# The sample's MLP up-projection with seven block products instead of eight, summed in PSUM

## The chip, the cores and the metric

The kernel runs on one NeuronCore of a Trainium2 chip. The metric is the device time of one execution in microseconds (us). The kernel before takes 2704.45 us (median of 3 runs, 2704.23 to 2707.36). The execution that the profiler recorded took 2709.24 us, of which 2707.5 us lie between its first and its last instruction.

## The reference

One encoder layer is applied to two sequences, a prompt of 512 tokens and a sample of 1024 tokens, with the same weights. Each sequence goes through an input projection, three token mixers, an output projection and an MLP. The change concerns the MLP of the sample alone:

```
D_MODEL, D_FF = 1024, 4096
def rmsnorm(x, w):
    return x * rsqrt(mean(x * x) + EPS) * w
...
x = x + mix @ w_out                                  # output projection
h = rmsnorm(x, norm_mlp_w)
x = x + square(relu(h @ w_up)) @ w_down              # the MLP
...
return rmsnorm(x, norm_f_w)                          # at the end of the trunk
```

All tensors are float32.

## The kernel before

**Products.** A float32 product is made of three passes: each operand is split into a high part (a copy rounded to the type `fp32r`) and a low part (the rest), and `unit` adds high x high, high x low and low x high into one PSUM tile of 128 x 512. Features lie on the partitions, tokens along the row; the sample's 1024 tokens are two blocks `b` of 512. One output tile with 1024 input features takes 8 x 3 = 24 matmuls of 128x512, one with 512 input features 12.

**Weights.** `wtile` loads 512 KB (or 256 KB) of weights by a DMA from the SyncE queue (SP) into a tile `wst` (two buffers), and `piece` splits each 128 x 512 quarter megabyte into a tile `w` (six buffers): ScalarE (ACT) writes the high part, VectorE (DVE) or GpSimd (POOL) the low part.

**The MLP before** (`tail`). After the output projection (tiles `op`, operands `m`) the residual x stands in `x2`. `norm_split` multiplies x by the norm's weight and splits it into eight operands `h` for each block; the factor 1/rms (`rr`, tiles `nacc`, `nsq`, `nps`) is not in them, it is multiplied in later. Then eight rounds `fb` follow: four up-projection tiles (`mu`) for each block, each 24 matmuls; `relu2` and `split` turn each into an operand `a`; and eight down-projection tiles (`md`) for each block, 12 matmuls each, are added onto x by DVE. In the last round the second block is done in two halves of 256 tokens, so that the final norm overlaps.

**Order.** Code records operations with a serial number; a planner (`schedule`) then lets every engine, whenever it is free by the planner's own costs, take the ready operation with the lowest number (`key`). The result is one fixed order for each engine, and each engine runs it strictly in that order, waiting on semaphores. Operations that need a buffer become ready only when one of its ring is free: `q4` (36 buffers of 128 x 1024; x, `h`, `m`, `a`), `w`, `wst`, `e` (11 buffers of 128 x 512 for intermediate results), and the PSUM rings `d` (3 banks) and `m` (5 banks).

The profile names one helper line for nearly every instruction (L592 before, L593 in the changed kernel), so groups are told apart by the tile names.

Of the kernel before, what the change touches and what calls it, by code (L numbers as in the profile page):

```python
# [9 lines left out]
F32 = mybir.dt.float32  # L10
F32R = mybir.dt.float32r
# [5 lines left out]
P = 128  # L17
D = 1024
KT = 8
# [3 lines left out]
WHOLE, HALVES = (slice(0, 512),), (slice(0, 256), slice(256, 512))  # L23
XN = 7
QN = 18
GDN_SHARE = 0.75
FIRST = 8


# [566 lines left out]
def kernel(ctx, tc, xp_t, xs_t, w_in, w_out, w_up, w_down, par, up, out_p, out_s):  # L596
    rec = Rec()
# [19 lines left out]
    def dram(shape, name):  # L617
        return V.of(Buf(name, shape, F32, real=dp.tile(list(shape), F32, name=name)))
# [25 lines left out]
    def mm(o, l, r, start=True, stop=True, **kw):  # L644
        PE.matmul(o, l, r, start=start, stop=stop, **kw)
# [4 lines left out]
    def copy(o, i, **kw):  # L650
        ACT.activation(o, i, AF.Copy, **kw)

    def tt(e, o, a, b, op):
        e.tensor_tensor(o, a, b, op=op)
# [3 lines left out]
    def stt(o, a, sc, b, op0, op1):  # L658
        DVE.scalar_tensor_tensor(o, a, sc, b, op0=op0, op1=op1)
# [38 lines left out]
    def mkseq(name, x, out, n):  # L698
        s = Seq()
        s.name, s.x, s.out, s.n = name, x, out, n  # L700
        s.C, s.nb = n // P, n // 512
        s.raw = [dram([P, n], f"raw_{name}_{g}") for g in range(NG)]
        s.mix = [dram([P, n], f"mix_{name}_{g}") for g in range(16)]
        s.lsd = [dram([P, n], f"lsd_{name}_{h}") for h in range(4)]
        s.rbs = [dram([P, n], f"rbs_{name}_{g}") for g in range(2)]
        s.cumd = dram([64, n], f"cumd_{name}")
        s.shr = [dram([P, s.C, 2, P], f"shr_{name}_{h}") for h in range(4)]
        s.pkd = [[dram([P, s.C, 4, P], f"pkd_{name}_{h}_{d}") for d in range(2)] for h in range(4)]
        s.nd = [[dram([P, s.C, P], f"nd_{name}_{h}_{d}") for d in range(2)] for h in range(4)]
        s.zt = [dram([2, s.C, 4, 32, 32], f"zt_{name}_{h}") for h in range(4)]  # L710
        s.xt = [dram([2, s.C, 4, 32, 32], f"xt_{name}_{h}") for h in range(4)]
        s.et = const([P, 4, 2, s.C], f"et_{name}")
        s.colt = const([P, s.C, 4, 24], f"col_{name}")
        s.ecol = const([P, s.C, 2, 8], f"ecol_{name}")
        s.neg = const([P, s.C, 2, 4], f"neg_{name}")
        return s


    def piece(src, ring="w"):
        w = rec.tile(ring, [P, 2, 512], F32R, "w")  # L720
        split(src, w, ANY)
        return w

    def wtile(src, nk=KT, ring="w"):
        st = rec.tile("wst", [P, nk * P], F32, "wst")
        SP.dma_start(st, src)
        return [piece(st[:, k:k + 512], ring) for k in range(0, nk * P, 512)]

    def split(src, hl, e):
        copy(hl[:, 0, :], src)  # L730
        tt(e, hl[:, 1, :], src, hl[:, 0, :].bitcast(F32), SUB)
# [11 lines left out]
    def unit(ps, w, hs, nk=KT, z=slice(0, 512)):  # L743
        n = 0
        for k in range(nk):
            a, b = (w[k // 4][:, i, k % 4 * P:(k % 4 + 1) * P] for i in range(2))
            hh, hl = hs[k][:, 0, z], hs[k][:, 1, z]
            for l, r in ((a, hh), (a, hl), (b, hh)):
                mm(ps, l, r, n == 0, n == 3 * nk - 1)
                n += 1  # L750
# [11 lines left out]
    def rms(src, sums=((DVE, (0, 1, 2, 3, 4, 5, 6)), (DVE, (7,))), n=512):  # L762
        part = lambda name: tmp(name)[:, 0:n]
        acc = []
        for e, ks in sums:
            a = part("nacc")
            act(a, src(ks[0]), AF.Square)
            for k in ks[1:]:
                sq = part("nsq")
                act(sq, src(k), AF.Square)  # L770
                tt(e, a, a, sq, ADD)
            acc.append(a)
        ps = psd("nps")[:, 0:n]
        mm(ps, ones, acc[0], True, False)
        mm(ps, ones, acc[1], False, True)
        rsq(ps, acc[0], 1.0 / D, room=acc[1])
        return acc[0]

    def norm_split(src, wcol, r=None):
        out = []  # L780
        for k in range(KT):
            h = tmp("nh")
            if r is None:
                DVE.tensor_scalar(h, src(k), col(wcol + k), None, op0=MUL)
            else:
                stt(h, src(k), col(wcol + k), r, MUL, MUL)
            hl = rec.tile("q4", [P, 2, 512], F32R, "h")
            split(h, hl, ANY)
            out.append(hl)
        return out  # L790
# [628 lines left out]

    def tail(s):
        blk = range(s.nb)
        sl = lambda b: slice(b * 512, (b + 1) * 512)
        x2 = [[rec.tile("q4", [P, 2, 512], F32, "x2") for _ in range(4)] for _ in blk]
        xk = lambda b, k: x2[b][k // 2][:, k % 2, :]
        for hf in range(2):
            rbs, hh = [], []
            for b in blk:  # L1430
                if hf:
                    rbs.append(rec.tile("q4", [P, 2, 512], F32, "rb"))
                    for g in range(2):
                        SP.dma_start(rbs[b][:, g, :], s.rbs[g][:, sl(b)])
                hh.append([])
                for k in range(KT):
                    f = tmp("mf")
                    SP.dma_start(f, s.mix[hf * 8 + k][:, sl(b)])
                    if hf:
                        stt(f, f, hn[:, 2 + k:3 + k], rbs[b][:, k // 4, :], MUL, MUL)  # L1440
                    m = rec.tile("q4", [P, 2, 512], F32R, "m")
                    split(f, m, ANY)
                    hh[b].append(m)
            for og in range(KT):
                w = wtile(w_out[hf, og])
                for b in blk:
                    ps = psd("op")
                    unit(ps, w, hh[b])
                    if hf == 0:
                        SP.dma_start(xk(b, og), s.x[og, :, sl(b)])  # L1450
                    tt(DVE, xk(b, og), xk(b, og), ps, ADD)

        h2, rr = [], []
        for b in blk:
            h2.append(norm_split(lambda k: xk(b, k), C_NMLP))
        for b in blk:
            rr.append(rms(lambda k: xk(b, k)))
        ends = [(b, z) for b in blk for z in (HALVES if b else WHOLE)]
        for fb in range(8):
            acts = [[] for _ in blk]  # L1460
            for f in range(4):
                w = wtile(w_up[4 * fb + f])
                for b in blk:
                    ps = psd("mu")
                    unit(ps, w, h2[b])
                    r = tmp("mr")
                    relu2(r, ps, rr[b])
                    a = rec.tile("q4", [P, 2, 512], F32R, "a")
                    split(r, a, ANY)
                    acts[b].append(a)  # L1470

            parts = [[(b, WHOLE[0]) for b in blk]] if fb < 7 else [[e] for e in ends]
            ws = {}
            for part in parts:
                for og in range(KT):
                    if og not in ws:
                        ws[og] = wtile(w_down[fb // 2, og, :, fb % 2 * 512:fb % 2 * 512 + 512], nk=4,
                                       ring="q4" if fb == 7 and og >= 4 else "w")
                    for b, z in part:
                        ps = psd("md")[:, 0:z.stop - z.start]  # L1480
                        unit(ps, ws[og], acts[b], 4, z)
                        tt(DVE, xk(b, og)[:, z], xk(b, og)[:, z], ps, ADD)
        with shifted(-200):
            rs = [rms(lambda k: xk(b, k)[:, z], ((DVE, (0, 4, 1, 5, 2, 6)), (DVE, (3, 7))), z.stop - z.start) for b, z in ends]
        for (b, z), r in zip(ends, rs):
            n = z.stop - z.start
            for k in range(KT):
                v = xk(b, k)[:, z]
                DVE.tensor_scalar(v, v, col(C_NF + k), None, op0=MUL)
            for k in range(KT):  # L1490
                v = xk(b, k)[:, z]
                tt(ANY, v, v, r, MUL)
                if k % 2:
                    SP.dma_start(s.out[k - 1:k + 1, :, b * 512 + z.start:b * 512 + z.stop].rearrange("k p t -> p k t"),
                                 x2[b][k // 2][:, :, z])

    def relu2(r, z, rr):
        stt(r, z, 0.0, rr, ALU.max, MUL)
        act(r, r, AF.Square)
# [46 lines left out]
    with lane("mix"):  # L1546
# [2 lines left out]
            next(g)  # L1549
        for _ in turns((one_by_one(g, gdn(ss_)), GDN_SHARE), (one_by_one(others(sp_), others(ss_)), 1.0)):  # L1550
            pass
    tail(sp_)
    tail(ss_)

    order, _ = schedule(rec)
    left = ctx.enter_context(tc.tile_pool(name="left", bufs=1))
# [112 lines left out]
```

## Time and profile before

| | us |
|---|---|
| median of 3 runs | 2704.45 |
| the profiled execution | 2709.24 |
| its span, first to last instruction | 2707.5 |
| TensorE (PE) busy | 2588.8 (96%) |
| DVE busy | 1758.3 (65%) |
| ACT busy | 1344.5 (50%) |
| sample's MLP, from the first `mu` to the last matmul | 1993.8 to about 2697.5 |

A busy PE in this profile means that matmuls follow each other without a gap; a matmul's own duration is longer than the distance to the next, because they are pipelined. What one matmul costs is therefore read from the distance of starts. The clock in the rows is the TensorE clock that was granted, as a share of 2.4 GHz.

### The profile page before, as it was taken

The numbers are of one execution on the slowest core, as the hardware profiler recorded it, in microseconds if no ns is written. First come the engines' busy times: TensorE is split into PE (matmuls) and PEld (weight loads), VectorE is DVE, ScalarE is ACT, GpSimd is POOL, SyncE is SP. The second block draws the span as 40 slices with busy tenths as digits, with TensorE's granted clock in tenths as the row PEclk, the third lists the DMA queues.
The fourth block names the chain that finished last, engine by engine and source line by source line (L and its number), as shares of the span: only waits on it lengthen the run. The fifth ranks groups of instructions, "written<-read, shape, count | busy, mean of one in ns | idle before, by whom it ended". The sixth has DMA issues, their size and how long they took to land. (4 is left out here: it accounts for less than half of the span.)

```text
span 2707.5 us, 39889 instructions
## 1 busy us (share of the span) xinstructions
PE 2588.8 (96%) x13992; PEld 2080.0 (77%) x13992; DVE 1758.3 (65%) x3235; ACT 1344.5 (50%) x2691; POOL 319.8 (12%) x623
## 2 busy tenths in 40 slices
PE   8999999989999999999999999999999999999998
PEld 6778777767767777677787788888888888888887
DVE  7997557989885558788997576565543333333336
ACT  6863448878855348776656455442331222122222
POOL 0110002323231012223121000000000000000001
PEclk9999999999999999999999999999999999999999
DMA  6796667666654677677645563462111111111112
GB/s 227 235 294 198 194 187 234 190 198 193 182 184 136 199 225 224 197 224 227 193 128 154 176 186 105 148 229 89 55 39 47 55 47 43 51 51 51 47 47 71
DMA packets 271145, 403.60 MB, mean 149 GB/s; under 512 B 48480, under 2 KB 124384, under 8 KB 270944
## 3 DMA queue, kind: packets, MB, share of 16 engines
q1 hardware_dynamic: 270944, 401.05, 47.3%
q8 instruction: 111, 1.82, 0.3%
q14 instruction: 90, 0.74, 0.1%
HBM read 299.11 MB, written 101.84 MB: 148 GB/s over the span
## 5 line engine op out<-in xcount | busy, mean ns | idle before, releaser
L592 PE MATMUL ip<-h,w 128*128 128x512 f32 x3384 | 865.4, 405 | 10.3 <-ACT h L592 7.4
L592 PEld LDWEIGHTS ip<-h,w 128*128 128x128 f32 x3384 | 628.8, 191 | 156.5 <-issue 12.1
L592 ACT ACTIVATE w<-wst 128x512 fp32r<-128x512 f32 x508 | 318.8, 629 | 679.6 <-PE md L592 312.9
L592 PE MATMUL md<-a,w 128*128 128x512 f32 (+1 forms) x2400 | 542.4, 383 | 2.3 <-ACT a L592 2.0
L592 PE MATMUL mu<-h,w 128*128 128x512 f32 x2304 | 540.3, 393 | 0.0
L592 PEld LDWEIGHTS md<-a,w 128*128 128x128 f32 x2400 | 434.9, 188 | 89.5 <-ACT a L592 3.4
L592 PEld LDWEIGHTS mu<-h,w 128*128 128x128 f32 x2304 | 431.0, 188 | 90.4 <-issue 1.2
L592 DVE TENSOR_TENSOR w<-wst,w 128x512 fp32r<-128x512 f32 x503 | 352.9, 703 | 142.9 <-ACT w L592 141.1
L592 DVE TENSOR_TENSOR x<-x,md 128x512 f32<-128x512 f32 (+1 forms) x200 | 132.8, 665 | 226.7 <-PE md L592 226.0
L592 PE MATMUL op<-m,w 128*128 128x512 f32 x1152 | 268.4, 392 | 0.0
L592 PEld LDWEIGHTS op<-m,w 128*128 128x128 f32 x1152 | 214.9, 188 | 47.0 <-issue 2.6
L592 DVE SCALAR_TENSOR_TENSOR cy<-cx,taps,cy 128x512 f32<-128x512 f32 x264 | 202.5, 792 | 6.4 <-ACT cy L592 2.9
L592 DVE SCALAR_TENSOR_TENSOR mr<-mu,nacc 128x512 f32<-128x512 f32 x96 | 66.2, 690 | 154.5 <-PE mu L592 154.3
L592 POOL TENSOR_TENSOR x<-x,nacc 128x512 f32<-128x512 f32 (+1 forms) x11 | 13.4, 1245 | 1053.6 <-DVE nacc L592 1053.6
L592 ACT ACTIVATE mr<-mr 128x512 f32<-128x512 f32 x96 | 60.6, 631 | 152.8 <-DVE mr L592 148.6
L592 DVE TENSOR_TENSOR a<-mr,a 128x512 fp32r<-128x512 f32 x96 | 66.6, 695 | 75.7 <-ACT a L592 75.4
L592 POOL TENSOR_SCALAR_AFFINE_SELECT E<-E 128x512 f32<-128x512 f32 x96 | 78.6, 826 | 181.4 <-DMA E<-cumd_s 101.0
L592 ACT ACTIVATE E<-E,col_s 128x128 f32<-128x128 f32 x256 | 82.1, 392 | 27.0 <-POOL E L592 26.8
L592 ACT ACTIVATE ev<-ip 128x512 f32<-128x512 f32 x94 | 55.5, 591 | 60.0 <-PE ip L592 53.8
L591 ACT ACT_TABLE_LOAD x62 | 79.5, 1283 | 1.1
L592 DVE SCALAR_TENSOR_TENSOR S<-S,dec,ds 64x64 f32<-64x64 f32 x256 | 61.1, 280 | 11.1 <-ACT S L592 4.2
L592 DVE TENSOR_TENSOR x<-x,op 128x512 f32<-128x512 f32 x48 | 32.8, 683 | 54.3 <-PE op L592 54.2
(243 smaller groups left out, 3071.6 us busy)
## 6 DMA issues: line engine op xcount, KB each, us to landing
wst<-in_w_in_dram SPq DMA_DIRECT2D x94, 512.0 KB, 4.4
wst<-in_w_up_dram SPq DMA_DIRECT2D x64, 512.0 KB, 3.5
wst<-in_w_down_dram SPq DMA_DIRECT2D x128, 256.0 KB, 2.6
raw_s<-ev SPq DMA_DIRECT2D x94, 256.0 KB, 2.7
E<-cumd_s SPq DMA_DIRECT2D x64, 256.0 KB, 5.0
pk<-pkd_s SPq DMA_DIRECT2D x64, 256.0 KB, 4.0
wst<-in_w_out_dram SPq DMA_DIRECT2D x32, 512.0 KB, 3.6
raw_p<-ev SPq DMA_DIRECT2D x47, 256.0 KB, 2.4
```

Of the source, the lines that this page charges most:

```text
L591: nc.scalar.preload_act_table_set(o.load)
L592: getattr(getattr(nc, o.eng), o.meth)(*[conv(x) for x in o.args], **{k: conv(x) for k, x in o.kw.items()})
```

## The change

The sample's up-projection is done by a scheme of Strassen's kind. The operands of one pair of output tiles (`q`, 16 of them) are seen as a 2 x 2 block matrix on each side: the weights in output tiles 2q and 2q+1 and in input features 0 to 511 and 512 to 1023 (a11, a12, a21, a22), the activations in input features 0 to 511 and 512 to 1023 and in the two token blocks. Seven products of half the input features (12 matmuls each) take the place of eight. Sums and differences of the operands are made first: on the side of the activations once (`t1` to `t4`, beside the plain blocks `11`, `21` and `22`), on the side of the weights for each q (`s1`, `s2`, a21-a11, a12-s2).

Three PSUM tiles carry the products of one q. X takes the product 11, is copied out as `p1`, and then goes on adding the product 21. W takes t1, is read by DVE (W + p1), and goes on adding 22. Y takes t2, is read, goes on adding t3, is read, goes on adding t4, and is read. The four sums are output tiles and go to DRAM (`z`). For three q the part of X is done first (`AHEAD_Q`), while the operands t1 to t4 are still being made. The residual x goes to DRAM as well (`xr`), to free buffers. Afterwards `z` and `xr` are read back, `relu2` and `split` follow, and the down-projection runs in rounds of 8, 8, 8, 4 and 4 input tiles in place of eight rounds of 4. The output projection's loop takes the outputs in the order 0, 4, 1, 5, 2, 6, 3, 7. The prompt's tail stays as it was, in a function of its own.

```diff
+AHEAD_Q = 3
...
+        if s.nb == 2:
+            s.z = [dram([P, n], f"z_{name}_{f}") for f in range(32)]
+            s.xr = dram([8, P, n], f"xr_{name}")
...
-    def tail(s):
+    def out_proj(s, ogs=range(KT)):
...
-            for og in range(KT):
+            for og in ogs:
...
+        return x2, xk
...
-        for fb in range(8):
-            acts = [[] for _ in blk]
-            for f in range(4):
-                w = wtile(w_up[4 * fb + f])
-                for b in blk:
-                    ps = psd("mu")
-                    unit(ps, w, h2[b])
...
+    def tail_sample(s):
+        blk = range(2)
+        sl = lambda b: slice(b * 512, (b + 1) * 512)
+        x2, xk = out_proj(s, (0, 4, 1, 5, 2, 6, 3, 7))
+        wn = lambda k: col(C_NMLP + k)
+        h = {x: [] for x in ("11", "21", "t1", "t2", "t3", "22", "t4")}
+
+        def part(x, v, k=None):
+            hl = rec.tile("q4", [P, 2, 512], F32R, "h")
+            if k is None:
+                split(v, hl, DVE)
+            else:
+                copy(hl[:, 0, :], v, scale=wn(k))
+                stt(hl[:, 1, :], v, wn(k), hl[:, 0, :].bitcast(F32), MUL, SUB)
+            h[x].append(hl)
+
+        for k in range(4):
+            part("11", xk(0, k), k)
+            part("21", xk(0, k + 4), k + 4)
+
+        def prod(ps, w, x, first=False, last=False):
+            n = 0
+            for k in range(4):
+                a, b = (w[:, i, k * P:(k + 1) * P] for i in range(2))
+                hh, hl = h[x][k][:, 0, :], h[x][k][:, 1, :]
+                for l, r in ((a, hh), (a, hl), (b, hh)):
+                    mm(ps, l, r, first and n == 0, n == 11, skip_group_check=True)
+                    n += 1
+
+        def raw(f):
+            r = rec.tile("wst", [P, KT * P], F32, "wst")
+            SP.dma_start(r, w_up[f])
+            return r[:, 0:512], r[:, 512:1024]
+
+        def put(f, b, v):
+            SP.dma_start(s.z[f][:, sl(b)], v)
+
+        def corner(q, a11, a12):
+            X = psd("mu")
+            prod(X, piece(a11), "11", True)
+            p1 = tmp("p1")
+            copy(p1, X)
+            return p1, X
+
+        def corner2(q, X, a12):
+            prod(X, piece(a12), "21", last=True)
+            v = tmp("z")
+            copy(v, X)
+            put(2 * q, 0, v)
+
+        ahead = []
+        for q in range(AHEAD_Q):
+            a11, a12 = raw(2 * q)
+            p1, X = corner(q, a11, a12)
+            corner2(q, X, a12)
+            ahead.append(p1)
+
+        for k in range(4):
+            x11, t1, t2, t3, t4 = (tmp(x) for x in ("x11", "t1", "t2", "t3", "t4"))
+            copy(x11, xk(0, k), scale=wn(k))
+            stt(t1, xk(1, k), wn(k), x11, MUL, SUB)
+            part("t1", t1)
+            stt(t2, xk(1, k + 4), wn(k + 4), t1, MUL, SUB)
+            part("t2", t2)
+            tt(DVE, t3, x11, t2, SUB)
+            part("t3", t3)
+            part("22", xk(1, k + 4), k + 4)
+            stt(t4, xk(0, k + 4), wn(k + 4), t2, MUL, SUB)
+            part("t4", t4)
+        rr = [rms(lambda k: xk(b, k)) for b in blk]
+        for b in blk:
+            for k2 in range(4):
+                SP.dma_start(s.xr[2 * k2:2 * k2 + 2, :, sl(b)].rearrange("k p t -> p k t"), x2[b][k2])
+
+        for q in range(16):
+            a11, a12 = raw(2 * q)
+            a21, a22 = raw(2 * q + 1)
+            if q < len(ahead):
+                p1 = ahead[q]
+            else:
+                p1, X = corner(q, a11, a12)
+            s1, s2 = tmp("s1"), tmp("s2")
+            W, Y = psm([P, 512], "mu"), psm([P, 512], "mu")
+            tt(ANY, s1, a21, a22, ADD)
+            prod(W, piece(s1), "t1", True)
+            t, u = tmp("z"), tmp("z")
+            tt(DVE, t, W, p1, ADD)
+            tt(ANY, s2, s1, a11, SUB)
+            prod(Y, piece(s2), "t2", True)
+            tt(DVE, u, Y, p1, ADD)
+            if q >= len(ahead):
+                corner2(q, X, a12)
+            tt(ANY, a21, a21, a11, SUB)
+            prod(Y, piece(a21), "t3")
+            tt(DVE, t, Y, t, ADD)
+            put(2 * q + 1, 1, t)
+            tt(ANY, a12, a12, s2, SUB)
+            prod(W, piece(a12), "22", last=True)
+            tt(DVE, u, W, u, ADD)
+            put(2 * q, 1, u)
+            prod(Y, piece(a22), "t4", last=True)
+            tt(DVE, p1, Y, p1, ADD)
+            put(2 * q + 1, 0, p1)
+
+        x2 = [[None] * 4 for _ in blk]
+        xk = lambda b, k: x2[b][k // 2][:, k % 2, :]
+        ends = [(b, z) for b in blk for z in (HALVES if b else WHOLE)]
+        for f0, nf in ((0, 8), (8, 8), (16, 8), (24, 4), (28, 4)):
+            acts = []
+            for b in blk:
+                acts.append([])
+                for f in range(f0, f0 + nf):
+                    v = tmp("av")
+                    SP.dma_start(v, s.z[f][:, sl(b)])
+                    relu2(v, v, rr[b])
+                    a = rec.tile("q4", [P, 2, 512], F32R, "a")
+                    split(v, a, ANY)
+                    acts[b].append(a)
+
+            end = f0 == 28
+            groups = ([[(b, og, WHOLE[0]) for b in blk for og in (g, g + 1)] for g in range(0, KT, 2)] if not end else
+                      [[(b, og, z) for og in range(KT)] for b, z in ends])
+            ws = {}
+            for group in groups:
+                for b, og, z in group:
+                    if f0 == 0 and x2[b][og // 2] is None:
+                        x2[b][og // 2] = rec.tile("q4", [P, 2, 512], F32, "x2")
+                        SP.dma_start(x2[b][og // 2], s.xr[og:og + 2, :, sl(b)].rearrange("k p t -> p k t"))
+                    if og not in ws:
+                        ws[og] = wtile(w_down[f0 // 8, og, :, f0 % 8 * P:(f0 % 8 + nf) * P], nk=nf,
+                                       ring="q4" if end and og >= 4 else "w")
+                    ps = psd("md")[:, 0:z.stop - z.start]
+                    unit(ps, ws[og], acts[b], nf, z)
+                    tt(DVE, xk(b, og)[:, z], xk(b, og)[:, z], ps, ADD)
+        ending(s, x2, ends)
...
-    tail(sp_)
-    tail(ss_)
+    tail_prompt(sp_)
+    tail_sample(ss_)
```

Three places in the order of the engines show how the planner places this.

ACT around the end of the sample's output projection, before: the squares for the norm (`nsq`, `nacc`) stand between the splits of weights (`w`) and operands (`h`) that the last output tiles need.

```order
L592 ACTIVATE nsq_19972<-x_3507_18819 128x512
L592 ACTIVATE w_19984<-wst_19867 128x512
L592 ACTIVATE w_20000<-wst_19867 128x512
L592 ACTIVATE h_20006<-nh_19974 128x512
L592 ACTIVATE nsq_20012<-x_3511_18853 128x512
L592 ACTIVATE h_20023<-nh_20015 128x512
L592 ACTIVATE nacc_20048<-x_3507_18819 128x512
L592 ACTIVATE h_20055<-nh_20050 128x512
```

The same engine in the changed kernel, after the output projection; `mu_20178` is X of the third q done ahead, `w_20263` the high part of the first s1.

```order
L593 ACTIVATE p_3681_20214<-mu_20178 128x512
L593 ACTIVATE nsq_20216<-x_3505_18676 128x512
L593 ACTIVATE z_20231<-mu_20178 128x512
L593 ACTIVATE nsq_20239<-x_3506_18462 128x512
L593 ACTIVATE nsq_20242<-x_3506_18462 128x512
L593 ACTIVATE nsq_20245<-x_3507_18761 128x512
L593 ACTIVATE nacc_20247<-x_3507_18761 128x512
L593 ACTIVATE nacc_20250<-x_3508_18428 128x512
L593 ACTIVATE nsq_20253<-x_3508_18428 128x512
L593 ACTIVATE nsq_20255<-x_3509_18719 128x512
L593 ACTIVATE nsq_20260<-x_3509_18719 128x512
L593 ACTIVATE w_20263<-s_3744_20233 128x512
```

The squares have moved behind the output projection and behind X's copies, in one run, and the first split of s1 stands behind them.

PE at the same place, before: from the last output-projection tile to the norm's sums over partitions (`nps`) and the first up-projection tile.

```order
L592 MATMUL op_20040<-m_19435,w_19851 128x512 x3
L592 MATMUL nps_20076<-nacc_19518,ones 128x512
L592 MATMUL nps_20076<-nacc_20048,ones 128x512
L592 MATMUL nps_20085<-nacc_19557,ones 128x512
L592 MATMUL nps_20085<-nacc_20083,ones 128x512
L592 MATMUL mu_20096<-h_19525,w_19911 128x512 x3
```

PE in the changed kernel, from the end of X of the third q (60 matmuls behind the output projection up to there, then the twelve of its second product) to W (`mu_20268`) and Y (`mu_20299`) of the first q.

```order
L593 MATMUL mu_20178<-h_19621,w_20107 128x512 x3
L593 MATMUL mu_20178<-h_19775,w_20107 128x512 x3
L593 MATMUL mu_20178<-h_20020,w_20107 128x512 x3
L593 MATMUL mu_20178<-h_20079,w_20107 128x512 x3
L593 MATMUL nps_20257<-nacc_20172,ones 128x512
L593 MATMUL nps_20257<-nacc_20247,ones 128x512
L593 MATMUL mu_20268<-h_19598,w_20263 128x512 x3
L593 MATMUL mu_20268<-h_19751,w_20263 128x512 x3
L593 MATMUL mu_20268<-h_20046,w_20263 128x512 x3
L593 MATMUL mu_20268<-h_20091,w_20263 128x512 x3
L593 MATMUL mu_20299<-h_19669,w_20291 128x512 x2
L593 MATMUL nps_20305<-nacc_20250,ones 128x512
```

The norm's sums now stand between the products done ahead and the first W.

DVE in the middle of the up-projection, before: `relu2` of one tile, the low part of a weight piece, the low part of an operand `a`.

```order
L592 SCALAR_TENSOR_TENSOR mr_21330<-mu_21288,nacc_19557 128x512
L592 TENSOR_TENSOR w_21326<-wst_21268,w_21326 128x512
L592 TENSOR_TENSOR a_21342<-mr_21330,a_21342 128x512
L592 SCALAR_TENSOR_TENSOR mr_21364<-mu_21324,nacc_19518 128x512
L592 TENSOR_TENSOR a_21373<-mr_21364,a_21373 128x512
```

DVE in the changed kernel, twelve of the sixteen instructions of one q in the middle: `mu_20743` is W, `mu_20763` Y, `wst_20738` and `wst_20760` hold the weights of the next q.

```order
L593 TENSOR_TENSOR z_20769<-mu_20743,p_3803_20745 128x512
L593 TENSOR_TENSOR w_20765<-wst_20738,w_20765 128x512
L593 TENSOR_TENSOR z_20786<-mu_20763,p_3803_20745 128x512
L593 TENSOR_TENSOR s_3822_20791<-wst_20760 128x512
L593 TENSOR_TENSOR w_20782<-wst_20738,w_20782 128x512
L593 TENSOR_TENSOR s_3823_20799<-s_3822_20791,wst_20738 128x512
L593 TENSOR_TENSOR wst_20760<-wst_20760,wst_20738 128x512
L593 TENSOR_TENSOR wst_20738<-wst_20738,s_3823_20799 128x512
L593 TENSOR_TENSOR w_20808<-s_3822_20791,w_20808 128x512
L593 TENSOR_TENSOR z_20769<-mu_20763,z_20769 128x512
L593 TENSOR_TENSOR w_20823<-s_3823_20799,w_20823 128x512
L593 TENSOR_TENSOR z_20786<-mu_20743,z_20786 128x512
```

The readings of W and Y stand between sums and splits for the next q, and the one that splits the next a11 (`w_20765`) stands ahead of the first reading of Y.

Over the whole program the lists have 11,638 matmuls in place of 11,830, 3,390 DVE instructions in place of 3,237, 2,789 on ACT in place of 2,693 and 1,619 on SP in place of 1,496. PE's list is the same up to the first tile of the sample's output projection.

## Rows read from the trace of the kernel before

**Rows 1.** Page, part 1: busy us, share of the span, instructions.

```profile
PE 2588.8 (96%) x13992; PEld 2080.0 (77%) x13992; DVE 1758.3 (65%) x3235; ACT 1344.5 (50%) x2691; POOL 319.8 (12%) x623
```

**Rows 2.** Windows: us; busy PE, PEld, DVE, ACT, POOL; clock; DMA share; GB/s.

```profile
1900.00:1994.00 94.00, 94.00 (x411) 76.64 (x409) 48.68 (x79) 31.56 (x52) 0.00 (x0) 1.00 0.15 47
1994.00:2650.00 656.00, 656.00 (x2895) 543.01 (x2894) 252.10 (x370) 159.51 (x253) 0.00 (x0) 1.00 0.15 48
2650.00:2707.50 57.50, 45.64 (x288) 40.68 (x286) 42.21 (x90) 14.65 (x30) 10.07 (x9) 0.91 0.21 74
```

**Rows 3.** Waits of PE after 1700 us: total us, times, longest.

```profile
PE nps L592 <- DVE nacc L592: 1.9, 1, 1.9
PE md L592 <- ACT a L592: 1.2, 1, 1.2
```

**Rows 4.** Timeline of PE from 1900 us: start, duration, tiles, count.

```profile
1899.63 91.29 PE L592 MATMUL op<-m,w 128*128 128x512 f32 x402
1990.76 3.60 PE L592 MATMUL nps<-nacc,ones 128*128 128x512 f32 x8
...
2037.74 43.68 PE L592 MATMUL md<-a,w 128*128 128x512 f32 x192
...
2603.50 43.68 PE L592 MATMUL mu<-h,w 128*128 128x512 f32 x192
```

**Rows 5.** Groups of PE by form, 1994 to 2698 us: busy, mean ns, idle.

```profile
L592 PE MATMUL md<-a,w 128*128 128x512 f32 (+1 forms) x1632 | 352.5, 377 | 0.0
L592 PE MATMUL mu<-h,w 128*128 128x512 f32 x1536 | 349.9, 389 | 0.0
```

**Rows 6.** Groups of DVE by form, from 1800 us.

```profile
L592 DVE TENSOR_TENSOR w<-wst,w 128x512 fp32r<-128x512 f32 x158 | 109.1, 692 | 41.4 <-ACT w L592 41.2
L592 DVE TENSOR_TENSOR x<-x,md 128x512 f32<-128x512 f32 x126 | 86.6, 688 | 186.2 <-PE md L592 186.2
```

**Rows 7.** Groups of ACT by form, from 1800 us.

```profile
L592 ACT ACTIVATE nsq<-x 128x512 f32<-128x512 f32 x24 | 15.1, 631 | 41.9 <-DVE x L592 41.5
...
L592 ACT ACTIVATE nacc<-nps,eps 128x512 f32<-128x512 f32 x4 | 2.8, 690 | 2.8 <-PE nps L592 2.8
```

**Rows 8.** Timeline of DVE before the end of the output projection.

```profile
1981.74 0.68 DVE L592 TENSOR_TENSOR h<-nh,h 128x512 fp32r<-128x512 f32 x1
1982.34 0.68 DVE L592 TENSOR_TENSOR nacc<-nacc,nsq 128x512 f32<-128x512 f32 x1
1982.95 0.69 DVE L592 TENSOR_TENSOR h<-nh,h 128x512 fp32r<-128x512 f32 x1
...
1990.96 0.69 DVE L592 TENSOR_TENSOR x<-x,op 128x512 f32<-128x512 f32 x1 [1.37 <-PE op L592]
```

**Rows 9.** Timeline of ACT in the same stretch.

```profile
1980.75 0.64 ACT L592 ACTIVATE h<-nh 128x512 fp32r<-128x512 f32 x1
1981.29 0.62 ACT L592 ACTIVATE nsq<-x 128x512 f32<-128x512 f32 x1
1981.92 0.63 ACT L592 ACTIVATE h<-nh 128x512 fp32r<-128x512 f32 x1
```

**Rows 10.** DMA issues: queue, count, KB each, median us to landing.

```profile
wst<-in_w_up_dram SPq DMA_DIRECT2D x64, 512.0 KB, 3.5
...
raw_s<-ev SPq DMA_DIRECT2D x94, 256.0 KB, 2.7
...
mf<-mix_s SPq DMA_DIRECT2D x32, 256.0 KB, 5.6
```

**Rows 11.** Timeline of PE at 72 us.

```profile
72.15 0.66 PE L592 MATMUL tp<-ident,cy 128*128 128x128 f32 x4 [2.77 <-DVE cy L592]
72.56 3.60 PE L592 MATMUL ip<-h,w 128*128 128x512 f32 x8
```

**Rows 12.** Window at this place, columns as in rows 2.

```profile
72.00:76.00 4.00, 3.85 (x13) 3.08 (x14) 4.00 (x8) 4.00 (x11) 0.27 (x4) 0.59 0.47 165
```

More of the change, by code (lines that the diff above doesn't have):

```diff
@@ L1451, in tail, with ending @@
                     tt(DVE, xk(b, og), xk(b, og), ps, ADD)
-        h2, rr = [], []
-        for b in blk:
[L1455 to L1458, printed above, removed]
-        for fb in range(8):
-            acts = [[] for _ in blk]
-            for f in range(4):
-                w = wtile(w_up[4 * fb + f])
-                for b in blk:
-                    ps = psd("mu")
-                    unit(ps, w, h2[b])
[L1466 to L1482, printed above, removed]
+        return x2, xk
+    def ending(s, x2, ends):
+        xk = lambda b, k: x2[b][k // 2][:, k % 2, :]
         with shifted(-200):
@@ L1485, in tail @@
         for (b, z), r in zip(ends, rs):
-            n = z.stop - z.start
             for k in range(KT):
@@ L1495, in tail, with tail_prompt @@
                                  x2[b][k // 2][:, :, z])
+    def tail_prompt(s):
+        x2, xk = out_proj(s)
+        h2 = norm_split(lambda k: xk(0, k), C_NMLP)
+        rr = rms(lambda k: xk(0, k))
+        for fb in range(8):
+            acts = []
+            for f in range(4):
+                w = wtile(w_up[4 * fb + f])
+                ps = psd("mu")
+                unit(ps, w, h2)
+                r = tmp("mr")
+                relu2(r, ps, rr)
+                a = rec.tile("q4", [P, 2, 512], F32R, "a")
+                split(r, a, ANY)
+                acts.append(a)
+            for og in range(KT):
+                w = wtile(w_down[fb // 2, og, :, fb % 2 * 512:fb % 2 * 512 + 512], nk=4)
+                ps = psd("md")
+                unit(ps, w, acts, 4)
+                tt(DVE, xk(0, og), xk(0, og), ps, ADD)
+        ending(s, x2, [(0, WHOLE[0])])
@@ new lines, in tail_sample @@
+    def tail_sample(s):
[92 more added lines that the diff above has]
+        x2 = [[None] * 4 for _ in blk]
+        xk = lambda b, k: x2[b][k // 2][:, k % 2, :]
+        ends = [(b, z) for b in blk for z in (HALVES if b else WHOLE)]
+        for f0, nf in ((0, 8), (8, 8), (16, 8), (24, 4), (28, 4)):
+            acts = []
+            for b in blk:
[4 more added lines that the diff above has]
+                    relu2(v, v, rr[b])
+                    a = rec.tile("q4", [P, 2, 512], F32R, "a")
+                    split(v, a, ANY)
[16 more added lines that the diff above has]
+        ending(s, x2, ends)
```

## The prediction

> **What bounds the kernel now.** I read the page's shares first: PE 96% busy, DVE 65% [rows 1]. Then the windows of the sample's tail: from 1900 to 2650 us PE is busy for 750 us of 750, at full clock, while DVE works 252 of 656 us and ACT 160 [rows 2]. The waits say the same: after 1700 us PE waits 3.1 us in all [rows 3]. So in the stretch that is changed every matmul counts with its whole distance to the next, and an instruction on any other engine costs nothing until PE has to wait for it.
>
> The distance comes from the PE timeline: thirteen stages of 192 matmuls lie between the starts 2037.74 and 2603.50, so 565.76 / 2496 = 0.2267 us for one matmul, 2.72 us for one product of twelve [rows 4]. DVE takes 0.69 us for 128x512, but back to back its starts are 0.60 us apart; I use 0.65. ACT takes 0.63 us and starts every 0.54 to 0.63 us; I use 0.6 [rows 6, 7, 8, 9]. DVE begins on a tile right when its last matmul's record ends (1990.92, start 1990.96 [rows 4, 8]); a record is 0.39 us long for a distance of 0.23 [rows 5], so a reader starts about 0.2 us after the matmul's own slot. I take 0.2 for the way back too.
>
> **What is removed.** The sample's up-projection has 1536 matmuls [rows 5]: 64 tiles of 24. Seven products of 12 for each of 16 q make 1344. 192 x 0.2267 = **43.5 us** less on PE. The down-projection has as many matmuls as before, the output projection too, and the norm's four sums (3.60 us [rows 4]) stay. PE has no idle time here that could be won besides.
>
> **What is added off PE.** 153 more DVE instructions (106 us at 0.69) and 96 more on ACT (60 us) go into a stretch in which DVE is idle for 404 us and ACT for 496 [rows 2], so on the average they are covered; what counts is order. I take three places.
>
> *The loop, q 3 to 15.* A q takes PE 7 x 2.72 = 19.0 us and DVE 16 x 0.65 = 10.4. PE's order is X, W, Y, X, Y, W, Y. Between the end of a product that is read and the next use of its bank lies one other product, 2.72 us; reading takes 0.2 + 0.69 + 0.2 = 1.1. DVE must then be free at the right moment. Put Y(t2)'s end at 0: its reading is over at 0.9, six instructions stand before the reading of Y(t3), which ends at 5.4, and they are done at about 4.8; W's end at 8.2 and Y(t4)'s at 10.9 find DVE with two instructions behind it. Pieces for the next q are split 8 us or more before PE wants them. One instruction is delicate: the split of the next a11 stands ahead of Y(t2)'s reading. Its weights can load only when both `wst` buffers are free, about 13.4 us after the last Y(t2); with 3.5 us to landing [rows 10], a copy and the split it is done 18 to 18.6 us after that, and Y(t2) ends at 19.0. PE feels it only if the landing takes over 5.5 to 6 us. In the loop about 2 MB move in 19 us, 110 GB/s, where 165 were moved at 72 us [rows 12], so I take 0. The bounds: 0, and 1.1 us for each of 80 readings, 88 us, if no product hid any of them. The trace has no bank that goes on adding after a reading, so between these ends I go by the row of `x<-x,md`, where a PSUM tile is read beside other matmuls without a PE wait. A gain is excluded, since PE has nothing to give back.
>
> *The start of it.* Here the order shown with the change is bad. Put the output projection's last matmul at 0. The X of three q are 72 matmuls, 16.3 us. Before the last twelve PE needs ACT's copy `p1`, issued 0.2 us after the first twelve are done (13.6): 0.2 + 0.6 + 0.2, a wait of **1.0**; X ends at 17.3. Next on PE is the norm's sum, which needs all squares of block 0. Before, the squares stood between the output tiles, and PE never waited. Now four of them stand on ACT behind the copy of X that can start only at 17.5: the last is done at 18.1 + 4 x 0.6 = 20.5, DVE's addition at 20.6, PE goes on at 20.8: a wait of **3.4**. The sum takes 1.8, to 22.6. W needs `w_20263`, which stands behind four squares of block 1: 20.5 + 5 x 0.6 = 23.5, with 0.2 and the low part about 0.3 later: **1.4**. W ends at 26.7. Y needs a piece that is seven ACT instructions further on (one of them of 0.69 us [rows 7]): 23.5 + 4.3 = 27.8, again **1.3**. Two small ones for low parts, **0.7**. Together 7.8 us. The weights for the second q can be loaded only when those of the first are split, at about 32 us, which its W just bears.
>
> A wait of PE has a second price. At 72 us PE waited 2.77 us, and then eight matmuls took 3.60 us, 0.45 each, and the window's clock is 0.59 in the mean, so mostly the lower level [rows 11, 12]: 3.60 - 8 x 0.2267 = **1.8 us** more. I take one such dip behind the wait of 3.4. The bounds of this place: 0, if ACT and DVE run a little ahead of this, and 15 (half as much again, with two dips).
>
> *The way over DRAM.* 64 stores and 64 loads of 256 KB and eight and eight of x at 512 KB: the nearest rows are 2.7 us for a store and 5.6 us for a load in a busy stretch [rows 10]. The first round's values are stored over 100 us before they are wanted, and in the order six of the first eight operands `a` are split before the last two q. SP sends loads in order, so a load that waits for a buffer holds up the weights behind it; the second block's operands have 10.9 us of matmuls of the first before they are wanted. I take **1 us**; bounds 0 and 8 (one load of 5.6 and its four instructions exposed).
>
> **The sum**, against the profiled execution: 2709.24 - 43.5 + 7.8 + 1.8 + 1 = 2676.3. That execution lies 4.8 us above the median of the runs, 2704.45; the same difference, -32.9, gives 2671.5, so **2672 us**. With the start at 4 to 15 us it is 2666 to 2678.
>
> **Rivals.**
> *The start is hidden.* If the scheme's operands and squares come early enough, PE stays full: 2704.45 - 43.5 = 2661. For it: DVE and ACT start sometimes at 0.54. Against: the wait for X's copy is fixed by the order.
> *The loop waits for weights.* If the landing takes 7 to 7.5 us instead of 3.5, Y's reading slips by about 1.5 us in each of 13 q: 2672 + 20 = 2692. For it: 5.6 us has been seen, and stores share the queue; against it the 0.15 DMA share.
> *The clock falls in the loop.* If the short waits come in each q and each brings one dip of 1.8 us, 16 x 1.8 = 29 us go: 2701, no change. Against it: from 1900 to 2650 the clock is 1.00, but with no waits at all; it would take waits like that at 72 us, not of tenths.
> The Trainium skill ("TensorE: Matmul & The Clock Gate", A second HAM failure mode) tells of a kernel that cycled through PSUM banks, whose short PE idles between groups of matmuls made the clock swing; that would be this case, and the rows at 72 us agree that a wait is followed by the lower level, while no row here shows it for waits under a microsecond.
> *Slower.* The readings of W and Y are exposed: if DVE, in its fixed order, comes to each one late, every one of the 80 costs PE up to 1.1 us, 88 us: 2672 + 88 = 2760. It decides against the kernel from 32.9 / 16 = 2.1 us per q, two exposed readings of five. For it: the five readings stand among eleven other DVE instructions that wait for ACT and DMA in turn. Against: the slack counted above.
> *That it doesn't do what it says* is excluded by the lists: 11,638 matmuls for 11,830.
>
> **Chances.** Forecast 0.64, hidden start 0.13, late weights 0.14, clock 0.03, exposed readings 0.06. About 0.2% (5.4 us) is what a measurement can tell from no change. Faster takes the first three, 0.91; same the clock's, 0.03; slower 0.06. The range, 2661 to 2692, holds the forecast with its bounds, the hidden start and most of the late weights.
>
> **What would show it.** `mu` of the sample with 1344 matmuls, and 0.2267 us apart; PE waits of some 8 us between the output projection and the second q, named `nps` <- DVE `nacc` and `mu` <- ACT `w` or `p`; no PE waits from the fourth q to the last; a few tenths at the first `md`. Wrong would be a row of PE waits on DVE `z` or `p1` in every q, on `wst`, or on `av` loads; or a clock under 1 in the middle of the loop.

## The result and the profile after

The changed kernel takes 2670.94 us (median of 4 runs, 2664.66 to 2675.29), against 2705.9 us of the kernel before: the ratio is 0.9858, 95% interval 0.9827 to 0.9890. A second measurement of it gave 0.9881 (0.9859 to 0.9903). The profiled execution took 2672.08 us with a span of 2670.4 us; before it was 2709.24 and 2707.5.

The page's first part, to be read against [rows 1]:

```profile
PE 2549.2 (95%) x13800; PEld 2042.3 (76%) x13800; DVE 1849.6 (69%) x3388; ACT 1394.6 (52%) x2787; POOL 326.1 (12%) x626
```

192 matmuls are gone, and 153 instructions on DVE and 96 on ACT have come. The groups of PE by form from the end of the output projection to the end, with busy time, mean ns and idle time, answer to [rows 5]; the down-projection is split in two forms here:

```profile
L593 PE MATMUL md<-a,w 128*128 128x512 f32 x1440 | 326.6, 389 | 0.0
L593 PE MATMUL mu<-h,w 128*128 128x512 f32 x1344 | 308.4, 391 | 1.1 <-ACT p L593 0.7 <-DVE w L593 0.4
```

PE's timeline from the last output tiles to the second q answers to [rows 4] (start, duration, tiles, count, idle time ahead and what ended it):

```profile
1979.82 9.00 PE L593 MATMUL op<-m,w 128*128 128x512 f32 x39
1988.66 13.76 PE L593 MATMUL mu<-h,w 128*128 128x512 f32 x60
2003.11 3.01 PE L593 MATMUL mu<-h,w 128*128 128x512 f32 x12 [0.69 <-ACT p L593]
2009.65 3.78 PE L593 MATMUL nps<-nacc,ones 128*128 128x512 f32 x4 [3.52 <-DVE nacc L593]
2012.44 5.11 PE L593 MATMUL mu<-h,w 128*128 128x512 f32 x14
2017.39 1.88 PE L593 MATMUL nps<-nacc,ones 128*128 128x512 f32 x4
2018.70 8.91 PE L593 MATMUL mu<-h,w 128*128 128x512 f32 x36
2028.02 277.62 PE L593 MATMUL mu<-h,w 128*128 128x512 f32 x1222 [0.41 <-DVE w L593]
```

There are three waits, all ahead of the second q, and then 1222 matmuls without a wait that this view names. The windows (us; busy PE, PEld, DVE, ACT, POOL; clock; DMA share; GB/s), to be read against [rows 2], show the low clock behind the wait of 3.52 us and a full PE from there on:

```profile
2008.00:2016.00 8.00, 6.35 (x13) 3.76 (x14) 5.96 (x11) 6.48 (x13) 0.00 (x0) 0.57 0.05 17
2016.00:2030.00 14.00, 13.59 (x56) 9.87 (x55) 12.69 (x20) 5.13 (x10) 1.67 (x1) 1.00 0.32 109
2030.00:2300.00 270.00, 270.00 (x1191) 223.24 (x1190) 166.87 (x257) 91.35 (x153) 0.00 (x0) 1.00 0.41 138
2300.00:2600.00 300.00, 300.00 (x1325) 248.40 (x1324) 142.55 (x222) 94.84 (x159) 0.00 (x0) 1.00 0.30 101
```

What comes ahead of the change runs in the same order in both kernels, and yet ends at another time in each execution. So I compare a stretch instead of the whole: from the end of the sample's output projection on PE to the start of the last norm's sum. In the kernel before it runs from 1990.76 to 2696.40, 705.6 us; in the changed kernel from 1988.66 to 2659.51 (the row below), 670.9 us.

```profile
2659.51 1.29 PE L593 MATMUL nps<-nacc,ones 128*128 128x256 f32 x4 [1.90 <-DVE nacc L593]
```

The change in the stretch is -34.8 us: 43.5 us of matmuls less, and 8.7 us of losses more, nearly all at the start.

### The profile page after: what moved, and what is told of

It reads as the page before. It is cut to its first block, busy times and chain, and to the rows that moved or that the text cites. A ratio compares the mean times of both kernels' runs of the same rounds, so it can differ in the third digit from the quotient of the medians.

```text
span 2670.4 us, 40087 instructions
## 1 busy us (share of the span) xinstructions
PE 2549.2 (95%) x13800; PEld 2042.3 (76%) x13800; DVE 1849.6 (69%) x3388; ACT 1394.6 (52%) x2787; POOL 326.1 (12%) x626
## 5 line engine op out<-in xcount | busy, mean ns | idle before, releaser
L593 PEld LDWEIGHTS ip<-h,w 128*128 128x128 f32 x3384 | 627.8, 191 | 156.4 <-issue 12.1
L593 ACT ACTIVATE w<-wst 128x512 fp32r<-128x512 f32 x524 | 328.7, 629 | 630.5 <-PE md L593 232.3
L593 DVE TENSOR_TENSOR w<-wst,w 128x512 fp32r<-128x512 f32 x520 | 365.1, 704 | 215.6 <-ACT w L593 213.2
L593 PE MATMUL mu<-h,w 128*128 128x512 f32 x2112 | 498.6, 394 | 1.1 <-ACT p L593 0.7
L593 PEld LDWEIGHTS mu<-h,w 128*128 128x128 f32 x2112 | 395.5, 189 | 86.6 <-issue 1.7
L593 DVE TENSOR_TENSOR x<-x,md 128x512 f32<-128x512 f32 (+1 forms) x152 | 99.9, 658 | 160.4 <-PE md L593 159.6
L593 DVE TENSOR_TENSOR x<-x,op 128x512 f32<-128x512 f32 x48 | 32.9, 684 | 44.4 <-PE op L593 44.2
L593 PE MATMUL y<-Cx,S 128*64 128x128 f32 x384 | 56.1, 282 | 6.3 <-issue 3.8
L593 PE MATMUL y<-E,tok 128*64 128x128 f32 x384 | 59.3, 279 | 0.9 <-ACT w L593 0.5
L593 DVE SCALAR_TENSOR_TENSOR cy<-cx,cy 128x512 f32<-128x512 f32 x66 | 47.6, 729 | 17.9 <-ACT cx L593 17.6
```

The costliest lines, as they stand in the source:

```text
L593: getattr(getattr(nc, o.eng), o.meth)(*[conv(x) for x in o.args], **{k: conv(x) for k, x in o.kw.items()})
```

## The experiments

The stretch and PE's waits in it, ahead of the last norm's sum, for all kernels:

| kernel | stretch, from and to | us | waits | ratio of the times |
|---|---|---|---|---|
| before | 1990.76 to 2696.40 | 705.6 | none | |
| changed | 1988.66 to 2659.51 | 670.9 | 0.69, 3.52, 0.41 | 0.9858 |
| changed, again | 1991.75 to 2662.54 | 670.8 | 0.69, 3.52, 0.40 | 0.9881 |
| squares at the fourth q | 1990.04 to 2652.63 | 662.6 | none | 0.9852 |
| the same, again | 1996.98 to 2660.42 | 663.4 | 0.29 | 0.9864 |
| squares ahead of everything | 1986.94 to 2651.40 | 664.5 | 0.95, 0.50 | 0.9833 |
| eight products, over DRAM | 1990.35 to 2696.09 | 705.7 | none | 0.9985 |
| no X ahead | 1984.55 to 2653.61 | 669.1 | 4.18 | 0.9857 |
| late squares, no X ahead | 1983.70 to 2646.24 | 662.5 | none | |
| the same, again | 1993.80 to 2656.35 | 662.6 | none | 0.9834 |
| weights loaded twice | 1982.86 to 2647.19 | 664.3 | 1.75 | |
| 8 more DVE instructions per q | 1986.23 to 2649.54 | 663.3 | 0.30 | |
| 16 more DVE instructions per q | 1993.04 to 2667.74 | 674.7 | 5.5 in 7 places | |

**Squares at the fourth q.** My theory A was that the order at the start makes the losses; the rival B, that ACT and DVE are behind in total.

```diff
-        rr = [rms(lambda k: xk(b, k)) for b in blk]
         ...
         for q in range(16):
+            if q == 3:
+                rr = [rms(lambda k: xk(b, k)) for b in blk]
```

> The norm's squares and sums are recorded with the fourth q, not ahead of the first; nothing else differs from the changed kernel. Measure: the stretch of PE from the end of the sample's output projection to the start of the last norm's sum, 670.9 us in the changed kernel and 705.6 before, and PE's waits in it. Theory A (the order at the start: one run of squares on ACT ahead of the first s1, and the clock that falls behind that wait): the 3.5 us wait and the low clock (some 3 us) both go, the stretch is 663 to 665 us, the time some 6 us under the changed kernel. Rival B (ACT and DVE are behind in total, so that the squares only stand in another place): the waits come back in the first four q in other names, 3 us or more, and the stretch stays at 669 to 672.

PE's timeline in this kernel, from the output projection on:

```profile
1969.63 20.56 PE L593 MATMUL op<-m,w 128*128 128x512 f32 x90
1990.04 54.98 PE L593 MATMUL mu<-h,w 128*128 128x512 f32 x240
2044.86 1.02 PE L593 MATMUL nps<-nacc,ones 128*128 128x512 f32 x2
2045.31 3.31 PE L593 MATMUL mu<-h,w 128*128 128x512 f32 x12
2048.46 2.74 PE L593 MATMUL nps<-nacc,ones 128*128 128x512 f32 x6
2050.63 19.65 PE L593 MATMUL mu<-h,w 128*128 128x512 f32 x84
```

No wait is left, and the stretch is 662.6 us, 43.0 under that of the kernel before, where the matmuls alone make 43.5. B falls: the same work on ACT and DVE, with another number in the order, costs PE almost nothing. The whole time did not show it here (0.9852, interval 0.9828 to 0.9877), since its interval is wider than the difference.

**Squares ahead of the work done ahead.**

```diff
+        rr = [rms(lambda k: xk(b, k)) for b in blk]
         ahead = []
         for q in range(AHEAD_Q):
             ...
-        rr = [rms(lambda k: xk(b, k)) for b in blk]
```

> The norm's squares and sums are recorded ahead of the products done ahead and of t1 to t4, so that the squares again stand between the output tiles as in the kernel before. Theory A: PE's sums follow the output projection with a wait under 1.5 us, the clock stays up, the stretch is 663 to 666 us. Rival B: the operands t1 to t4 get late by what the squares take, PE waits 3 us or more for h or for the first W, the stretch is 669 us or more.

```profile
1986.94 3.60 PE L593 MATMUL nps<-nacc,ones 128*128 128x512 f32 x8
1989.97 14.94 PE L593 MATMUL mu<-h,w 128*128 128x512 f32 x62
2005.86 0.96 PE L593 MATMUL mu<-h,w 128*128 128x512 f32 x3 [0.95 <-DVE w L593]
2007.33 4.84 PE L593 MATMUL mu<-h,w 128*128 128x512 f32 x20 [0.50 <-ACT p L593]
```

The sums follow the output projection without a wait, as before the change; 1.45 us of waits stand at pieces and copies a little later, under a microsecond each. That they come late because of the squares ahead of them is argued, not shown. A holds, with a stretch of 664.5. The ratio is 0.9833 (0.9810 to 0.9855).

**Eight products, over DRAM.** The scheme is taken out and the rest left in:

```diff
+        h2 = [norm_split(lambda k: xk(b, k), C_NMLP) for b in blk]
+        rr = [rms(lambda k: xk(b, k)) for b in blk]
+        ...                                   # x to s.xr as in the changed kernel
+        for f in range(32):
+            w = wtile(w_up[f])
+            for b in blk:
+                ps = psd("mu")
+                unit(ps, w, h2[b])
+                v = tmp("z")
+                copy(v, ps)
+                SP.dma_start(s.z[f][:, sl(b)], v)
```

> The up-projection is the plain one of the kernel before, eight half products (1536 matmuls), but its outputs and x go over DRAM and the down-projection runs in rounds of 8, 8, 8, 4 and 4 as in the changed kernel: the DRAM way alone. Theory A: it hides, the stretch is that of the kernel before, 705 to 708 us, and the time is the same within the measurement; the scheme's 192 matmuls are then the whole gain. Rival C (the way over DRAM costs several us, and the scheme gains more than it seems): 710 us or more, with PE waits at the first md or for a.

The stretch is 705.7 us, 0.1 more than before, without a wait ahead of the last sum; the time is within 0.3% of it (0.9985, 0.9970 to 0.9999). So neither the stores and loads nor the other rounds of the down-projection cost or bring anything in the stretch, and the scheme alone makes the gain there.

**No X ahead.** `AHEAD_Q = 3` becomes 0.

> No X is done ahead (AHEAD_Q 0): PE has only the 24 matmuls of the first X, 5.4 us, while t1 to t4, the squares and the first s1 are made. Theory A (the start is bound by ACT's and DVE's order): PE waits 8 to 15 us there in place of 4.6, with the low clock behind it, the stretch is 676 to 684 us. Rival D (work done ahead plays no part, since PE waits for the norm's squares anyway): the waits stay at 4 to 6 us and the stretch at 670 to 673.

```profile
1984.55 2.88 PE L593 MATMUL mu<-h,w 128*128 128x512 f32 x12
1991.61 1.24 PE L593 MATMUL mu<-h,w 128*128 128x512 f32 x3 [4.18 <-ACT p L593]
1992.65 3.32 PE L593 MATMUL nps<-nacc,ones 128*128 128x512 f32 x4
1995.28 3.20 PE L593 MATMUL mu<-h,w 128*128 128x512 f32 x11
```

I was wrong: there is one wait of 4.18 us in place of 4.62 in three, and the stretch is 669.1 us, just under what D expected. ACT's timeline tells what PE waited for: four squares stand ahead of X's copy, which could have started at about 1987.5.

```profile
1987.58 0.61 ACT L593 ACTIVATE nsq<-x 128x512 f32<-128x512 f32 x1
1988.85 0.63 ACT L593 ACTIVATE nacc<-x 128x512 f32<-128x512 f32 x1 [0.66 <-DVE h L593]
1989.45 0.63 ACT L593 ACTIVATE nsq<-x 128x512 f32<-128x512 f32 x1
1990.17 0.63 ACT L593 ACTIVATE nacc<-x 128x512 f32<-128x512 f32 x1
1990.96 0.60 ACT L593 ACTIVATE p<-mu 128x512 f32<-128x512 f32 x1 [0.16 <-DVE nacc L593]
```

**Late squares and no X ahead.**

> Squares at the fourth q and no X done ahead. Theory A (the squares' place alone makes the waits at the start): PE waits for the copy of X, 0.7 to 1.5 us, and for s1, 0 to 2 us; the stretch is 663 to 666 us. Rival F (work done ahead covers t1 to t4): with 5.4 us of matmuls beside some 8 us of DVE and GpSimd work on t1 to t4 and s1, PE waits 4 us or more with a low clock behind it, the stretch is 668 us or more.

No wait, 662.5 us. So the work done ahead covers nothing that is needed: t1 to t4 are made in time behind 5.4 us of matmuls, and the squares' place alone makes the waits. F falls, and D was right that the work done ahead plays no part.

**Time of the two orders.** The changed kernel and the one with late squares were timed beside each other, the one with late squares and no X ahead by itself:

> The changed kernel once more, for its time beside the next one on the same chip. Theory A: 2668 to 2675 us, the stretch from the end of the output projection to the last norm's sum 670 to 672 us, with the same wait of some 3.5 us for the norm's sum and the same low clock behind it, since both follow from the order.

> The kernel with the norm's squares recorded at the fourth q once more, timed in five rounds. Theory A: stretch 662 to 664 us as before; time 5 to 10 us under the changed kernel run beside it, ratio to the kernel before 0.981 to 0.985. Rival E (what the stretch gains is given back ahead of it, where the two kernels have one and the same order): the two times agree within 2 us although the stretches differ by 8.

> Late squares and no X done ahead, the one with the least waits so far, timed in five rounds. Theory A: stretch 662 to 664 us (PE full: 705.6 less 43.5), time 2659 to 2668 us, ratio 0.981 to 0.985. If the stretch stays and the time does not, the rest is in what lies ahead of it.

The stretches come out as expected, 670.8, 663.4 and 662.6 us; the first two waits of the changed kernel are the same to 0.01 us in both executions. The times are 2673.61 (0.9881, 0.9859 to 0.9903), 2669.13 (0.9864, 0.9846 to 0.9883) and 2668.21 us (0.9834, 0.9820 to 0.9847). The median of the second lies 4.5 us under the first, less than the 5 to 10 expected, and the intervals overlap, so the whole times of these two orders are not told apart. In the profiled runs the one with late squares reached the end of the output projection 5.2 us later; whether that is chance or E's giving back, two runs do not show. The third kernel's interval is clear of the first's and overlaps the second's; its time of 2668.21 us lies just above the 2659 to 2668 expected.

**More work for DVE in the loop.** At four places in each of the q 4 to 14 (based on the late squares) 2 or 4 additions of 128x512 are made whose results nothing reads:

```diff
+        def pad(q, src, n):
+            if 4 <= q < 15:
+                dm = tmp("dm")
+                for _ in range(n):
+                    tt(DVE, dm, src, src, ADD)
```

> The kernel with the late squares, and eight more additions of 128x512 on VectorE in each of the q 4 to 14, whose results nothing reads: 24 in place of 16 instructions, about 15 of 19 us. Theory A (between a product that is read and the next use of its bank lies another product, so readings hide until DVE is full): no PE wait in the loop, the stretch stays at 662 to 665 us. Rival G (DVE's fixed order is already at its limit, and every further instruction makes readings late): waits of PE on DVE z in every q, 0.5 us or more each, the stretch 668 us or more.

> As with the eight more additions on VectorE for each q, but sixteen: 32 instructions in a q 4 to 14, 19.5 to 20.8 us at 0.61 to 0.65 us each, against 19.05 us of matmuls. Theory A (readings hide until VectorE is full): VectorE becomes the bound, PE waits 5 to 25 us over the eleven q on VectorE's z, p or w, the stretch is 668 to 690 us. Rival G (each reading is exposed as soon as VectorE is busy): 5 readings of 1.1 us in each q, 60 us, the stretch over 710 us.

Windows of the middle of the loop in the two kernels, 8 more first (columns as above):

```profile
2100.00:2260.00 160.00, 160.00 (x708) 132.49 (x707) 129.67 (x198) 48.07 (x81) 10.98 (x8) 1.00 0.40 134
```

```profile
2100.00:2260.00 160.00, 157.08 (x679) 125.25 (x678) 159.06 (x247) 42.46 (x72) 23.90 (x13) 1.00 0.36 117
```

With DVE at 130 us of 160 PE has no wait there; with DVE at 159 of 160 PE loses 12.1 us in the stretch (674.7 - 662.6), 1.1 us per q; the records name 5.5 us of it as waits, in seven places, all for pieces of weights (`w`) and none for a reading. The longest has the low clock behind it (0.66 in the mean from 2293 to 2298 us):

```profile
2293.26 20.59 PE L593 MATMUL mu<-h,w 128*128 128x512 f32 x82 [2.61 <-DVE w L593]
```

A holds and G falls. In part the planner gave splits to GpSimd (11 and 24 us busy), so the two kernels differ from the base by a little more than the additions.

**Weights loaded twice.**

```diff
             SP.dma_start(r, w_up[f])
+            if 8 <= f < 30:
+                SP.dma_start(r, w_up[f])
```

> Late squares, no X done ahead, and for the q 4 to 14 each 512 KB of the up-projection's weights is loaded twice into the same tile, one load behind the other, so that they land some 4 us later. The planner then sets the split of the next a11 behind the reading of Y. Theory A (pieces are split 8 us or more ahead of PE, and readings no longer stand behind the load): no PE wait, stretch 662 to 665 us. The rival of late weights: PE waits of 1 to 2 us in each of 11 q, the stretch at 675 us or more.

The stretch is 664.3 us, with one wait of 1.75 us, where A expected none. DVE's order tells where it comes from:

```profile
2250.18 0.69 DVE L593 TENSOR_TENSOR s<-wst 128x512 f32<-128x512 f32 x1 [2.64 <-DMA wst<-in_w_up_dram]
2250.79 0.68 DVE L593 TENSOR_TENSOR w<-wst,w 128x512 fp32r<-128x512 f32 x1
2251.39 0.68 DVE L593 TENSOR_TENSOR z<-mu,z 128x512 f32<-128x512 f32 x1
```

```profile
2252.13 41.09 PE L593 MATMUL mu<-h,w 128*128 128x512 f32 x180 [1.75 <-DVE z L593]
```

The sum s1 for the next q waits 2.64 us for weights that land late, while loads for the down-projection run beside; the reading of Y stands two instructions behind it, and PE waits for the reading before it goes on with Y. This is the rival of late weights, at one of eleven q and at another place in the order, since the planner had moved the split of a11 behind the reading. What late weights would do in the changed kernel's own order is not shown.

There the delicate place held. Three of the first readings of Y:

```profile
2085.35 0.69 DVE L593 TENSOR_TENSOR z<-mu,p 128x512 f32<-128x512 f32 x1 [1.36 <-PE mu L593]
2104.39 0.69 DVE L593 TENSOR_TENSOR z<-mu,p 128x512 f32<-128x512 f32 x1 [0.62 <-DMA wst<-in_w_up_dram]
2123.43 0.69 DVE L593 TENSOR_TENSOR z<-mu,p 128x512 f32<-128x512 f32 x1 [1.36 <-DMA wst<-in_w_up_dram]
```

Where the view names a load, the load is not what held the reading: from 2066.31 to 2256.71 these readings are 19.04 us apart, which is PE's time for seven products, and each begins 0.04 us after Y's last record ends. DVE was idle ahead of nearly all of them; the least room was 0.22 us at 2237.67 and none at 2256.71, when work for the down-projection had begun.

## Why the prediction was right

The sum was 2672 us and the median 2670.94. By its terms:

- **43.5 us of matmuls**: right. Late squares without X ahead save 705.6 - 662.6 = 43.0 us of the stretch, and with the eight products left in nothing is saved.
- **The loop at 0**: right. PE is busy for 270 of 270 us at clock 1.00. The reason given, that another product lies between a reading and the next use of the bank, is supported by the test with DVE at 130 of 160 us. The rival of exposed readings had a price of 88 us; even with DVE full the loss was 12.1 us, and the waits named in it are for pieces of weights.
- **The start at 7.8 us of waits and 1.8 us of low clock**: the place and the names were right and the sum was near (9.6 us, against 8.7 lost), but the split of it was not. The wait for the copy was 0.69 us (I had 1.0), for the norm's sum 3.52 (3.4), for a low part 0.41 (0.7). The waits for s1 (1.4) and for Y's piece (1.3) did not come, and the low clock cost more than 1.8 us: the norm's sum and the fourteen matmuls behind it took 7.74 us from start to start, where four records 0.43 us apart (worked out below, at the norm's sums) and 14 x 0.2267 make 4.89, so 2.85 us more. While PE was that slow, ACT caught up: `w_20263` was split on ACT at 2010.81, before PE came to W. The step that failed is that I added waits and low clock as if they were independent. That 2.7 us too much and 1.05 us too little stood side by side is in part why the sum came out so near, and that is luck. The 1.8 itself was a little high: the 3.60 us of [rows 11] contain the last record's own length, and up to the next start, the line at 75.96 of the kernel before, it is 3.40 - 1.81 = 1.6 us.

```profile
75.96 0.49 PE L592 MATMUL l2p<-cs,onesr 128*128 128x512 f32 x1
```

```profile
2006.16 0.60 ACT L593 ACTIVATE z<-mu 128x512 f32<-128x512 f32 x1 [2.58 <-PE mu L593]
2006.65 1.66 ACT L593 ACTIVATE nsq<-x 128x512 f32<-128x512 f32 x3
2008.21 1.14 ACT L593 ACTIVATE nacc<-x 128x512 f32<-128x512 f32 x2
2009.25 1.66 ACT L593 ACTIVATE nsq<-x 128x512 f32<-128x512 f32 x3
2010.81 0.62 ACT L593 ACTIVATE w<-s 128x512 fp32r<-128x512 f32 x1
```

These rows of the changed kernel show the run of squares as the order had it: it begins behind X's copy at 2006.16, and s1's split is last.

The starts on PE's timeline account for the whole loss. Over their matmuls at 0.2267 us, and 1.72 us for each sum of the norm, the stretches from 1988.66, 2003.11, 2009.65 and 2017.39 to the next of these starts, the last to 2028.02, take 0.85, 3.82, 2.85 and 0.75 us more, which is 8.3. A wait costs a little more here than the view's figure, because the view counts it from the end of a record. The remaining 0.4 us is spread over the 1222 matmuls behind, which take 277.45 us for 277.03.

- **The norm's pair of sums at 1.8 us**: right, though the reading was loose. I took half of the 3.60 us of [rows 4], which contains the last record's own length; eight records take 3.60 us and two take 1.02 (the kernel with squares at the fourth q), so they start (3.60 - 1.02) / 6 = 0.43 us apart, and a pair of sums takes 4 x 0.43 = 1.72 us. It moved nothing, as both kernels have the same sums.
- **DRAM at 1 us**: 0.1, by the kernel with eight products. The loads of `z` took 4.9 us to landing in the median and 8.4 at most, under the 10.9 us that cover them.
- **The clock in the loop**: right. The low level stands behind the wait of 3.52 us, and no wait came in the loop to bring another. With sixteen more DVE instructions there are waits of 0.38 to 0.65 us in the loop, and the clock stays at 1.00 from 2100 to 2260 us.
The Trainium skill ("TensorE: Matmul & The Clock Gate", A second HAM failure mode) tells of a clock that swings when PSUM banks are cycled with short idles between the groups. Here three PSUM tiles for each q are cycled for 277 us without such idles and the clock is 1.00, so cycling alone did not bring it; idles as frequent as that section has in mind were not tried.

The start and the way over DRAM were together put 1.8 us too high, which is nearly the whole distance between the forecast change of 32.9 us and the 34.8 us of the stretch. That the time agrees to 1 us is luck: the changed kernel's two medians, 2670.94 and 2673.61, lie further apart.

The rival of a hidden start (2661 us) was not what happened, but it is what one line of another order makes of this kernel: 662.6 us of stretch.

Open is what late weights would cost in the changed kernel's own order.

## What to carry to other kernels

Where one engine is full, a scheme that takes instructions from it gains just their distance from start to start, if the engines that get more work have room for it and each use of a result that another engine must read in between has a whole independent piece of work in front of it. The loss is then at the seam: look in the engines' order for a run of work that nobody needs yet (here the norm's squares, needed some 200 us later) ahead of the first thing the full engine waits for, and give it a later place. When the whole time scatters by as much as the effect, compare the stretch between two landmarks in the profile.

## What the runs showed beyond this

The part ahead of the change has the same order in all these kernels, and yet the output projection ended between 1982.86 and 1996.98 us, for one and the same kernel at 1983.70 and 1993.80. The mean granted clock over the span explains it in part at most. The latest and the earliest run of all, in this order (span, clock):

```profile
core 0: 2671.3 us, clock 0.985
```

```profile
core 0: 2658.1 us, clock 0.991
```

0.006 of some 2665 us are 16 us of full clock, against a difference of 14.1 us at the end of the output projection. But the one kernel at 1983.70 and 1993.80 us has 0.989 and 0.988, which would make 3 us of the 10; of the first 1900 us its PE was busy for 1797.4 in one execution and 1792.1 in the other, so the waits there differ too. What makes the scatter stays open.
